# Aligning the entry of three engine programs to an instruction block, in a kernel that streams 268 MB

## The chip, the cores and the metric

One core of a Trainium2 chip. The metric is the device time of one execution in microseconds (us); a kernel is given by the median of its fast executions. The span of a profile runs from the first to the last instruction and is about 1.8 us shorter than the time.

## The reference

```python
B, S, D = 8, 2048, 4096          # x: (8, 2048, 4096) f32, w: (4096, 1) f32

def reference(x, w):
    proj = (x @ w).squeeze(-1)                    # (8, 2048)
    cm = np.maximum.accumulate(proj, axis=1)
    is_record = (proj >= cm).astype(np.float32)
    return np.cumsum(is_record, axis=1).astype(np.float32)
```

So 268 MB of x are read once, each row is reduced to one number, and two short scans follow.

## The kernel before

The first 1920 positions of each batch row are loaded in 32 large pieces (four groups of eight), the last 128 in smaller ones, by SyncE, into a ring of three SBUF buffers of 64 KB per partition. VectorE takes columns 0 to 2815 of each row (multiply and add up in one instruction), Pool multiplies the other 1280 columns and ACT adds them up. TensorE broadcasts w to all partitions at the start and turns the sums into rows; VectorE scans them. VectorE, Pool, ACT and TensorE run the first three groups as a hardware loop of their own (`Fori`).

```python
    with tc.tile_critical(no_gpsimd_drain=True):
        for g in range(NG):
            r = RS[g]
            for t in range(B):
                i = SY.dma_start(out=at(g, t)[:, : r * D], in_=x[...]).then_inc(xs[t], 16)
                u, n = user_before(g, t)
                if n:
                    i._wait_ge(*(free(u, n)))      # the buffer's last user, VectorE and ACT
                if g == t == 0:
                    A.dma_start(                   # w, 16 KB, issued by ACT
                        out=w_row, in_=w.rearrange("(k c) one -> k (c one)", k=NW)
                    ).then_inc(ws, 16)
        # ... cut: stores of the counts, loads of the last 128 positions, constants (Pool), broadcast of w (TensorE, ACT)

        def group_dots(r, g=0):                    # VectorE
            for t in range(B):
                b, xb = B - 1 - t, at(g, t)
                for j in range(r):
                    i = dot(xb[:, j * D : j * D + VC], w_v[:, :VC], sum_v[...])
                    if j == 0:
                        i._wait_ge(xs[t], 16)
                i.then_inc(fr[t], 1)

        with V.Fori(0, NL):
            group_scans()
            V.sem_inc(psr, -3)
            group_dots(R)
        # ... cut: the like loops of Pool, ACT and TensorE, and the tail
```

## Time and profile before

| | before |
|---|---|
| time, three runs | 630.11 us (630.03 to 630.29) |
| span of the profiled run | 629.3 us |
| first x packet starts / last x packet ends | 1.98 / 623.76 us |
| from there to the end | 5.5 us |
| VectorE / Pool / ACT busy | 65% / 59% / 29% |

The profiled run took 631.05 us and so was itself 0.9 us slower than the median; its span should not be compared with others to better than a microsecond.

The page of before: the busy share of the DMA engines in 40 slices of the span (in tenths), and the queues with packets, MB and their share of the time of 16 engines.

```profile
span 629.3 us, 1140 instructions
...
DMA  9999999999999999999999999999999999999996
...
q1 hardware_dynamic: 6544, 268.50, 98.9%
...
q14 instruction: 3, 0.02, 0.0%
```

All 16 DMA engines are busy from the first slice to the last but one: the stream of x is the time. The line q14 counts the instruction blocks that the engines fetched while the kernel ran; three in the whole span.

The waits of before (who waited for whom: us in total, times, longest):

```profile
POOL xall L276 <- DMA xall<-in_x_dram: 243.3, 31, 20.9
DVE xall L124 <- DMA xall<-in_x_dram: 181.8, 30, 7.9
```

The two busiest engines wait for data some thirty times, once per piece.

The timeline of before, first 27 us (start, duration, engine, line, operation, then in brackets the idle time before it and what ended it):

```profile
0.91 0.60 ACTq L178 DMA_DIRECT2D w<-in_w_dram  x1
0.96 0.20 POOL L208 MEMSET identity<- 128x128 f32 x1 [0.51 <-SPq L163]
0.97 1.34 SPq L168 DMA_DIRECT2D xall<-in_x_dram  x3
...
2.62 2.07 PE L224 MATMUL ps<-w,identity 8*128 8x512 f32 x2 [2.62 <-DMA w<-in_w_dram]
...
18.31 0.48 DVE L246 MEMSET ps<- 8x512 f32 x1 [15.71 <-ACT w L235]
...
22.80 3.09 DVE L124 CUSTOM_DVE_ANT_0 xall<-xall,w_v 128x2816 f32<-128x2816 f32 x1 [0.67 <-DMA xall<-in_x_dram]
```

ACT issues w's load just ahead of SyncE's first x load (0.91 against 0.97 us), w's packets are through by 2.10 us, and the first dot is released by the data of x.

The end of the chain of work that ended last (start, duration, what):

```profile
581.81 39.25 DMA xall<-in_x_dram
621.06 0.07 issue
621.13 1.76 POOL xall L336
...
626.10 0.27 DVE cnt L146
```

The last 5 us are the last piece's sums and scans; none of the "issue" steps there is longer than 0.07 us.

### The profile page before, as it was taken

To read this page: it belongs to the slowest core of one execution; us is meant where nothing else is said; L and a number is where in the kernel's file an instruction comes from. 1 tells how busy PE (TensorE), PEld (TensorE's weight loads), DVE (VectorE), ACT (ScalarE), POOL (GpSimd) and SP (SyncE) were. 2 spreads that over 40 slices of the span, in tenths; PEclk is the share of its full clock that TensorE was granted. 3 is DMA by queue.
4 is the path that set the end of the run, shared out by engine and by line. 5 is a ranking of instruction groups with operands and counts; after the bars stand their busy time and mean duration, and the time that the engine had idled before them with its cause. 6 is when DMAs were issued, how large, how long until landed. Compare 5 with 4: busy or idle time off the path is not lost. (4 is left out here: it accounts for less than half of the span.)

```text
span 629.3 us, 1140 instructions
## 1 busy us (share of the span) xinstructions
PE 29.1 (5%) x96; PEld 13.5 (2%) x96; DVE 407.3 (65%) x294; ACT 181.2 (29%) x274; POOL 370.7 (59%) x149
## 2 busy tenths in 40 slices
PE   8000000000020000000001000000002000000100
PEld 3000000000010000000000000000001000000000
DVE  0755775556766567755578655676556976655897
ACT  1222332223322233222233222332223232232254
POOL 0554675456765557745577555676557666555775
PEclk9999999999999999999996555555555555555565
DMA  9999999999999999999999999999999999999996
GB/s 401 400 467 400 446 421 425 442 437 429 442 425 450 417 450 417 459 408 458 408 458 408 458 408 458 408 459 408 462 418 438 416 447 441 413 447 444 404 425 248
DMA packets 6563, 268.54 MB, mean 427 GB/s; under 512 B 760, under 2 KB 1016, under 8 KB 1568
## 3 DMA queue, kind: packets, MB, share of 16 engines
q1 hardware_dynamic: 6544, 268.50, 98.9%
q10 hardware_dynamic: 16, 0.02, 0.0%
q14 instruction: 3, 0.02, 0.0%
HBM read 268.45 MB, written 0.07 MB: 427 GB/s over the span
## 5 line engine op out<-in xcount | busy, mean ns | idle before, releaser
L124 DVE CUSTOM_DVE_ANT_0 xall<-xall,w_v 128x2816 f32<-128x2816 f32 (+1 forms) x129 | 385.5, 3041 | 181.8 <-DMA xall<-in_x_dram 181.8
L276 POOL TENSOR_TENSOR xall<-xall,w_sb 128x1280 f32<-128x1280 f32 x120 | 345.0, 2909 | 246.7 <-DMA xall<-in_x_dram 243.3
L130 ACT ACTIVATE xall<-xall 128x1280 f32<-128x1280 f32 (+2 forms) x130 | 162.9, 1253 | 428.6 <-POOL xall L276 408.3
L312 PE MATMUL ps<-identity,small 128*8 128x128 f32 x60 | 13.0, 406 | 568.6 <-PEq L309 568.6
L130 ACT ACTIVATION_READ_ACCUMULATOR xall<-xall 128x1 f32 x130 | 24.2, 186 | 0.0
L336 POOL TENSOR_TENSOR xall<-xall,w_sb 128x1280 f32<-128x1280 f32 (+2 forms) x8 | 21.1, 2632 | 3.1 <-DMA xall<-in_x_dram 3.0
L312 PEld LDWEIGHTS ps<-identity,small 128*8 128x8 f32 x60 | 7.3, 125 | 575.4 <-issue 571.3
L140 DVE TENSOR_TENSOR_SCAN cm<-ps,cm,small 8x512 f32<-8x512 f32 (+3 forms) x8 | 7.0, 869 | 18.8 <-PE ps L312 18.4
L224 PE MATMUL w_v<-w,identity 8*128 8x512 f32 x14 | 12.1, 1056 | 0.0
L124 DVE DVE_READ_ACCUMULATOR2_ANT small<- 128x1 f32 x133 | 10.8, 81 | 0.0
L246 DVE MEMSET ps<- 8x512 f32 x1 | 0.5, 485 | 15.7 <-ACT w L235 15.7
L146 DVE TENSOR_TENSOR_SCAN cnt<-ps,cnt,small 8x512 f32<-8x512 f32 (+3 forms) x8 | 7.0, 870 | 0.3
L224 PEld LDWEIGHTS w_v<-w,identity 8*128 8x128 f32 x14 | 4.6, 332 | 7.3 <-issue 7.3
L143 DVE TENSOR_TENSOR ps<-ps,cm 8x512 f32<-8x512 f32 (+3 forms) x8 | 3.9, 487 | 0.3
L232 ACT COPY w_sb<-w_v 128x768 f32<-128x768 f32 x1 | 0.8, 799 | 11.4 <-PE w_v L224 11.4
L347 POOL TENSOR_TENSOR masked<-fold,small 128x4 f32<-128x4 f32 x8 | 1.6, 201 | 3.2 <-DVE small L124 3.2
L124 DVE CUSTOM_DVE_ANT_0 xall<-xall,w_v,small 128x480 f32<-128x480 f32 (+2 forms) x4 | 3.1, 810 | 0.2 <-DVE small L124 0.2
L357 PE MATMUL ps<-fold,masked 128*8 128x32 f32 x20 | 2.0, 235 | 25.3 <-ACT masked L352 17.7
L352 ACT ACTIVATE masked<-fold,small 128x4 f32<-128x4 f32 x10 | 3.0, 298 | 0.3
L336 POOL TENSOR_TENSOR xall<-xall,w 128x640 f32<-128x640 f32 (+1 forms) x2 | 2.3, 1137 | 0.1
L224 PE MATMUL ps<-w,identity 8*128 8x512 f32 x2 | 2.1, 1135 | 2.6 <-DMA w<-in_w_dram 2.6
L231 ACT ACT_TABLE_LOAD x1 | 1.3, 1283 | 2.7 <-DVE fold L242 2.7
(18 smaller groups left out, 5.3 us busy)
## 6 DMA issues: line engine op xcount, KB each, us to landing
xall<-in_x_dram SPq DMA_DIRECT2D x8, 6144.0 KB, 33.5
xall<-in_x_dram SPq DMA_DIRECT2D x6, 2048.0 KB, 42.4
xall<-in_x_dram SPq DMA_DIRECT2D x1, 1264.0 KB, 36.6
xall<-in_x_dram SPq DMA_DIRECT2D x1, 816.0 KB, 39.3
xall<-in_x_dram SPq DMA_DIRECT2D x1, 784.0 KB, 37.9
xall<-in_x_dram SPq DMA_DIRECT2D x2, 240.0 KB, 26.6
xall<-in_x_dram SPq DMA_DIRECT2D x1, 416.0 KB, 39.4
xall<-in_x_dram SPq DMA_DIRECT2D x24, 45.0
```

What stands on the lines that cost most here:

```text
L124: return V.tensor_tensor_reduce(out=xsl, in0=xsl, in1=wsl, scale=1.0, scalar=seed, op0=ALU.mult, op1=ALU.add, accum_out=dst,)
L130: return A.activation(out=xsl, in_=xsl, func=ACTF.Copy, accum_out=dst)
L140: V.tensor_tensor_scan(out=cm_, data0=src, data1=low, initial=cm0, op0=ALU.max, op1=ALU.max,)._wait_ge(psr, base).then_inc(psr, 1)
L143: V.tensor_tensor(out=src, in0=src, in1=cm_, op=ALU.is_ge)._wait_ge(psr, base + 1).then_inc(psr, 1)
L146: V.tensor_tensor_scan(out=cnt_, data0=src, data1=low, initial=cnt0, op0=ALU.add, op1=ALU.max,)._wait_ge(psr, base + 2).then_inc(cs, 1)
L224: i = T.matmul(out=dst, lhsT=identity[:NW, k : k + 1].to_broadcast([NW, P]), rhs=w_row, start=True, stop=True,).then_inc(bw, 1)
L276: i = G.tensor_mul(out=xl, in0=xl, in1=w_sb).then_inc(pl, 1)
L312: i = T.matmul(out=ps[:B, j : r * P : r], lhsT=l[:, j * B : (j + 1) * B], rhs=identity, start=k == 0, stop=k == 1,)
L336: G.tensor_mul(out=xl, in0=xl, in1=w_pool(*p))._wait_ge(xq[i], 16).then_inc(pl, 1)
L347: return eng.tensor_tensor(out=e, in0=by_b, in1=acc.to_broadcast([P, H]), op=ALU.mult)
L352: return A.activation(out=e, in_=by_b, func=ACTF.Copy, scale=acc)._wait_ge(pa, na).then_inc(ms, 1)
L357: return T.matmul(out=ps[:B, k * Q : (k + 1) * Q], lhsT=masked[:, n * B : (n + 1) * B], rhs=by_i, start=start, stop=stop,)
```

## The change

The intent: let each engine's loop body lie inside one block of 128 instructions, with a fixed slot for the entry, so that neither back edges nor the tail meet an instruction fetch. `addr_align(128, 2, max_nops=0)` puts the next instruction at slot 2 of a block, by a branch over the gap.

```diff
     def free(u, n):
         return (p7, n) if u == B - 1 else (fr[u], 2 * n)
+
+    for eng in (V, A, G):
+        eng.addr_align(128, 2, max_nops=0)
 
     with tc.tile_critical(no_gpsimd_drain=True):
```

V, A and G are VectorE, ACT and Pool. SyncE and TensorE are left as they were. No other instruction changes; line numbers after it grow by 3.

## The prediction

> **What bounds the kernel now.** The stream of x. The page gives 268.45 MB read in a span of 629.3 us, and every slice but the last has the DMA row at 9. In the trace's packets the first x packet starts 1.98 us after the span's start, the last ends at 623.76 us, and between 2.5 and 622.8 us no 100 ns have fewer than 14 packets in flight on 16 engines. So the time is 2.0 us (entry) + 621.8 us (stream) + 5.5 us (tail: last sums, scans, output, exit). VectorE is busy 65%, Pool 59%, ACT 29%; their waits are for data. The timeline shows slack: the first tile lands at 22.8 us, its buffer is reloaded from 35.8 us, but two more 8.4 MB loads (some 19.5 us each) are then queued, so a buffer may come back over 20 us later before the queue runs dry.
>
> **What the change does.** It moves no arithmetic, load or wait. The VectorE, ACT and Pool programs get one padding instruction ahead of the entry branch, so these three jump to slot 2 of the next block of 128 instructions. The intent: each loop body (about 70, 75 and 36 slots) lies in one block.
>
> *Gain.* No back edge before shows a fetch stall: inside the span the instruction queue carried three 8 KB fetches (at 105.3, 117.4 and 487.6 us, 0.31 us each), none per iteration. There is nothing to save on the path.
>
> *Cost.* One taken branch per engine at about 0.75 us. The Trainium skill, "Runtime: NRT & Kernel Launch", section "Instruction fetch mechanics", says a branch stalls where the target lies outside the current two-page window. The next block should be inside. I read the three fetches as "entering a block fetches the one after", which agrees (the page has 16 KiB blocks, the trace 8 KB packets). So I expect 0.05 to 0.4 us per jump; if the block is missing, 1 to 3 us.
>
> *Critical path.* SyncE does not jump and does not wait for the three: its entry event precedes their branches, and it issues the first x load at 0.97 us. The stream starts at the same time. A late ACT delays the load of w (issued at 0.91 us), w's broadcast, and the first VectorE scans (ending at 22.1 us, 0.7 us ahead of the first tile). Even 3 us there only delays the first dot, and the slack swallows it. In the tail, Pool's program then lies in one block; VectorE and ACT cross once, near the end of the last group, with the block fetched ahead.
>
> **Predicted time:** 630.1 us, 8 in 10 between 629.5 and 630.9. Faster by over 2%: 0.3%; within 2%: 99%; slower by over 2%: 0.7%.
>
> **What would show the steps right.** Span within 0.5 us of 629.3; x stream 1.98 to about 623.8 us; first x load at 0.97 us; w load, copies of w and first dot later by under 0.5 us; three new 8 KB instruction fetches in the first 3 us, none in the loops, then one about 570 to 582 us (ACT) and one about 585 to 598 us (VectorE). Tail chain of the same pieces, 5.5 us. Wrong: the first x load late, a gap in the DMA row, or an "issue" wait of 1 us or more in the last 6 us.
>
> **What would make it wrong.** The jumped-to block is absent and its fetch takes many microseconds behind the x stream; w's load, issued after x has filled the queues, takes over 20 us; the new crossing stalls in the tail; the stream's rate differs on the chip used.

## The result, and the profile after

630.66 us (median of 4 runs, 630.45 to 631.17) against 630.16 us for the kernel before (now 4 runs, 630.03 to 630.29). The ratio is 1.0009, with a 95% interval from 0.9992 to 1.0026: no difference is shown.

The page after:

```profile
span 628.8 us, 1143 instructions
...
DMA  9999999999999999999999999999999999999995
...
q14 instruction: 5, 0.04, 0.0%
```

The three added instructions are the three branches. Five blocks were fetched in the span, where there had been three.

The timeline after, first 32 us:

```profile
0.96 2.12 SPq L171 DMA_DIRECT2D xall<-in_x_dram  x3
1.34 0.20 POOL L211 MEMSET identity<- 128x128 f32 x1 [0.89 <-SPq L166]
1.35 2.38 ACTq L181 DMA_DIRECT2D w<-in_w_dram  x1
...
11.14 2.07 PE L227 MATMUL ps<-w,identity 8*128 8x512 f32 x2 [11.14 <-DMA w<-in_w_dram]
...
26.84 0.48 DVE L249 MEMSET ps<- 8x512 f32 x1 [23.86 <-ACT w L238]
...
30.58 3.05 DVE L124 CUSTOM_DVE_ANT_0 xall<-xall,w_v 128x2816 f32<-128x2816 f32 x1
```

SyncE's first load is issued at the same time as before (0.96 us). ACT now issues w's load 0.4 us later, its issue lasts 2.38 us instead of 0.60, and w arrives 8.5 us later (first broadcast matmul at 11.14 against 2.62 us). The first dot moves from 22.80 to 30.58 us. It is no longer released by x but simply follows the scans.

The waits after, and the end of the chain:

```profile
POOL xall L279 <- DMA xall<-in_x_dram: 218.2, 30, 7.9
DVE xall L124 <- DMA xall<-in_x_dram: 172.9, 28, 7.3
...
DVE ps L249 <- ACT w L238: 23.9, 1, 23.9
```

```profile
581.46 39.13 DMA xall<-in_x_dram
620.60 0.07 issue
620.66 1.75 POOL xall L339
...
625.63 0.27 DVE cnt L146
```

VectorE waits 8.2 us longer for w (23.9 against 15.7 us) and 8.9 us less for data of x (172.9 against 181.8 us): what it lost at the start it took from its own idle time. The x stream ran from 2.00 to 623.29 us, and the end follows 5.5 us later, as before.

The instruction fetches and entry branches, read from the records of the two traces (us from the span's start):

| | before | after |
|---|---|---|
| entry branch: Pool, ACT, VectorE | 0.77, 0.77, 0.79 | 1.15, 1.20, 1.36 |
| added branch: Pool, ACT, VectorE | none | 0.70, 0.74, 0.77 |
| 8 KB fetches | 105.3, 117.4, 487.6 | 1.78, 1.80, 1.95, 559.8, 568.6 |

### The profile page after: what moved, and what is told of

The parts are those of the page before. It is cut to its first block, busy times and chain, and to the rows that moved or that the text cites. A ratio compares the mean times of both kernels' runs of the same rounds, so it can differ in the third digit from the quotient of the medians.

```text
span 628.8 us, 1143 instructions
## 1 busy us (share of the span) xinstructions
PE 29.3 (5%) x96; PEld 13.6 (2%) x96; DVE 407.1 (65%) x294; ACT 181.2 (29%) x274; POOL 370.6 (59%) x149
## 5 line engine op out<-in xcount | busy, mean ns | idle before, releaser
L124 DVE CUSTOM_DVE_ANT_0 xall<-xall,w_v 128x2816 f32<-128x2816 f32 (+1 forms) x129 | 385.4, 3040 | 172.9 <-DMA xall<-in_x_dram 172.9
L249 DVE MEMSET ps<- 8x512 f32 x1 | 0.5, 485 | 23.9 <-ACT w L238 23.9
```

Source lines behind the costliest of these rows:

```text
L124: return V.tensor_tensor_reduce(out=xsl, in0=xsl, in1=wsl, scale=1.0, scalar=seed, op0=ALU.mult, op1=ALU.add, accum_out=dst,)
```

## The experiments

Twelve kernels ran, all of them correct. The 630.66 against 630.16 asked whether half a microsecond had been lost, and the late w asked why.

Theory: the x stream sets the time, the three jumps lie beside it, and whatever they delay is taken from slack. Rivals: the jumps or the late w cost a little that the first runs could not show; the block layout itself matters.

### The changed kernel again

No edit. 

> The changed kernel unaltered, in more rounds, to settle whether its 0.5 us over the kernel before (630.66 against 630.16) is real. Theory (the jumps lie off the path): within 0.05% of before, 630.0 to 630.6 us, x stream from 2.0 us, 621 to 622 us long. Rival (the jumps or the late load of w cost time): 0.08% slower or more, every round the same sign.

Measured: 630.49 us (five runs, 630.40 to 630.92) against 630.31 us (nine runs, 630.11 to 630.89); ratio 1.0002 [0.9988, 1.0016]. The theory's range holds the median, and the runs of the two kernels overlap. No cost of the change is shown; one of 0.1% is not excluded.

### ACT jumps after it has issued w's load

```diff
-    for eng in (V, A, G):
+    for eng in (V, G):
         eng.addr_align(128, 2, max_nops=0)
...
                     A.dma_start(out=w_row, ...).then_inc(ws, 16)
+                    A.addr_align(128, 2, max_nops=0)
```

> VectorE and Pool jump as in the change; ACT jumps only after it has issued the load of w. Theory (w is late because its load was issued at 1.35 us, after the first x load at 0.97 us, and its packets then queue behind x): w issued at 0.9 us, its packets landed by 2.3 us, first broadcast matmul at 2.6 to 3.1 us, as before; time 630.0 to 630.6. Rival (the jump itself delays w): first broadcast matmul near 11 us still. If the 0.5 us of the change came from the late w it is gone here.

Measured: 630.56 us, ratio 1.0003 [0.9989, 1.0017].

```profile
0.92 0.60 ACTq L181 DMA_DIRECT2D w<-in_w_dram  x1
```

w's load was issued at 0.92 us in 0.60 us, the first broadcast matmul came at 3.80 us (0.7 us later than expected; its packets took until 2.84 us in place of 2.10). So w is late because of where its issue stands, not because of VectorE's and Pool's jumps. And an early w does not make the kernel faster: the late w was not the cause of the half microsecond. These runs do not show that it is more than noise.

### w late without any jump

```diff
                 if g == t == 0:
+                    A.wait_ge(con, 7)
                     A.dma_start(out=w_row, ...)
```

> The kernel before without any jump; ACT waits for the constants (about 1.95 us) and only then issues the load of w. Theory (order behind x, not the jump): first broadcast matmul at 9 to 13 us, copies of w at 24 to 27 us, no instruction fetch in the first 20 us, time 630.0 to 630.6. Rival (fetches of instructions hold the load up): first broadcast matmul at 4 us.

Measured: 630.27 us, ratio 0.9997 [0.9983, 1.0011].

```profile
2.03 0.59 ACTq L179 DMA_DIRECT2D w<-in_w_dram  x1
```

ACT issued w at 2.03 us in 0.59 us; the first matmul came at 10.89 us, and there was no fetch in the first 100 us. Being issued behind the first x load is enough to make 16 KB take over 8 us. The trace shows how: w's packets started at 7.57 us, and the short packets that report them done only at 10.06 to 10.28 us, about one x packet (2.42 us) later. The Trainium skill, "DMA: Bandwidth & Descriptors", section "Queues, rings and completion order", says that each DMA engine takes turns between its queues and drains a whole packet before it switches; that agrees with the second step. The first one is 5.5 us from the issue to the packets. In the trace w's packets start when the engines end their second x packet (7.57 to 8.02 us), so two x packets went ahead of w; why two and not one is open.

### Only ACT jumps

```diff
-    for eng in (V, A, G):
+    for eng in (A,):
```

> Only ACT jumps. Theory: one instruction fetch of 8 KB at 1.5 to 2.2 us in place of three, ACT's entry branch at 1.2 us (0.43 us later than before), VectorE's and Pool's at 0.77 to 0.79 us as before; w still late, first broadcast matmul at 9 to 13 us. Of the late fetches one at 555 to 575 us is ACT's; VectorE and Pool keep two of the three of before. Span 628.3 to 629.5.

Measured (one run, state unknown): 630.24 us, span 628.4 us. One fetch near the start (1.80 us), ACT's entry branch at 1.20 us, VectorE's and Pool's at 0.79 and 0.77; first matmul at 10.85 us. The late fetches came at 104.5, 486.9 and 568.5 us: the last is ACT's, and so the one that is gone (117.4 us) was ACT's before. All as expected, but for one thing. ACT's issue of w took 2.28 us here, with no other engine jumping:

```profile
1.35 2.28 ACTq L181 DMA_DIRECT2D w<-in_w_dram  x1
```

That suggested that an engine's first load after it enters a block is held up by that engine's own fetch. It is not simply a wait for the fetch: its packet was done at 2.47 us, and the issue ended at 3.63 us. It matters for the engine that starts the stream.

### SyncE jumps as well

```diff
-    for eng in (V, A, G):
+    for eng in (SY, V, A, G):
```

> SyncE jumps as well. Theory (a jump costs 0.4 to 0.6 us and matters only on the engine that starts the stream of x): first x load issued at 1.35 to 1.5 us instead of 0.97, first x packet at 2.35 to 2.55 us, stream 621 to 622 us, tail 5.5 us, so the span 0.4 to 0.6 us above the changed kernel's, 630.7 to 631.1 us. ACT now issues w about as early as SyncE issues x, so the first broadcast matmul comes at 3 to 5 us again. Rival (jumps cost nothing, the delays of the other engines had other causes): x issued at 0.97 us.

Measured: 633.37 us, ratio 1.0045 [1.0031, 1.0059]: 3.1 us slower, not 0.5. SyncE issued its first x load at 1.46 us, as expected, but the issue took 2.51 us instead of 0.40, and the first x packet started at 4.58 us. The stream (621.6 us) and the tail (5.5 us) kept their lengths. The direction was right: on this engine a jump costs the whole kernel. The size was not: I had counted the jump and left out the fetch.

### SyncE alone jumps, to a new block and inside its block

```diff
-    for eng in (V, A, G):
-        eng.addr_align(128, 2, max_nops=0)
+    SY.addr_align(128, 2, max_nops=0)        # the first of the two kernels
+    SY.addr_align(128, 100, max_nops=0)      # the second, in its place
```

> Only SyncE jumps to the next block. Theory (the first load that an engine issues right after entering a block waits for that engine's own 8 KB fetch): SyncE's first x load is issued near 1.46 us and its issue takes 2.2 to 2.7 us instead of 0.40, first x packet at 4.3 to 4.8 us, time 632.6 to 633.5 us. ACT's issue of w takes 0.6 us. Rival (the four fetches of four engines and ACT's stretched issue crowd it): issue 0.4 to 0.8 us, first x packet at 2.4 to 2.9 us, time 630.7 to 631.3.

> Only SyncE jumps, but to slot 100 of the block that it is in, so no new block is entered. Theory (the fetch costs, not the branch): no fetch by it in the first 3 us, first x load issued at 1.05 to 1.25 us, issue 0.40 us, first x packet 2.05 to 2.25 us, time 630.3 to 630.8. Rival (any jump ahead of the first load costs 2 to 3 us): 632.5 us or more.

Measured: into a new block 632.32 us, ratio 1.0029 [1.0015, 1.0043]; inside the block 630.43 us, ratio 0.9999 [0.9985, 1.0012]. With the new block the first load was issued at 1.46 us, its issue took 1.85 us, and the first x packet started at 3.93 us. The start of the issue is as expected; the other two are a little under it (and the time too), but nearer to the theory than to the rival. ACT, which did not jump, issued w in 0.60 us, as expected. The fetch's packet was done at 2.12 us and SyncE's issue ended at 3.31 us, so what fills the time between is not shown. Inside the block there was no fetch at the start, the issue took 0.40 us, and x started at 2.20 us. So the branch costs 0.2 us and entering the new block the rest. The difference to the kernel where four engines jump (1.85 against 2.51 us) says that the fetches also crowd one another, or ACT's load crowds SyncE's; which, is open.

The stretch from 2 to 4 us, first of the kernel where SyncE alone enters a new block, then of before (window, length, busy us of PE, PEld, DVE, ACT, POOL, granted clock, DMA share, GB/s):

```profile
2.00:4.00 2.00, 0.97 (x1) 0.49 (x2) 0.57 (x2) 0.81 (x1) 0.42 (x6) 1.00 0.63 205
```

```profile
2.00:4.00 2.00, 1.38 (x2) 0.82 (x3) 0.57 (x2) 1.28 (x1) 0.00 (x0) 1.00 1.44 492
```

205 GB/s against 492: the first packets of x are missing. (A share over 1 comes from packets that overlap on an engine.)

### Two blocks ahead

```diff
     for eng in (V, A, G):
         eng.addr_align(128, 2, max_nops=0)
+        eng.addr_align(128, 1, max_nops=0)
```

> Each of the three jumps twice, to slot 2 of the next block and from there to slot 1 of the block after. Theory (the next block is there at entry, the one after is fetched only when the next is entered): the second jump waits for the 8 KB fetch of 1.8 to 2.4 us, entry branches at 2.3 to 3.5 us; w's load lands at 9 to 12 us; the x stream still starts at 2.0 us and the time is 630.0 to 630.7. Rival 1 (a jump costs its branch alone, wherever it goes): entry branches at 1.6 to 1.9 us. Rival 2 (the missing block is fetched behind x): 5 to 10 us.

Measured: the second jumps ended at 3.45 (ACT), 3.52 (Pool) and 3.80 us (VectorE), 2.3 to 2.5 us after the first ones. So the next block was there at entry, and the one after had to be fetched (at 1.8 us). ACT's issue of w then took 6.0 us, w landed at 17.2 us (9 to 12 had been expected), and the first dot came at 37.06 us. But the time was 631.26 us, ratio 1.0015 [1.0002, 1.0029]: 0.97 us slower, where I had expected nothing. The x stream started on time (1.98 us) and lasted 621.89 us, with the tail at 5.5 us. (The profile of before has 621.8 us, but that run was 0.9 us slow; the other kernels that kept their time have 620.9 to 621.3 us.) The late w is not it: an experiment below has a later first dot (39.8 us) at no cost. Near the end of the stream:

```profile
622.50:623.70 1.20, 0.00 (x0) 0.00 (x0) 1.20 (x3) 0.66 (x1) 1.11 (x2) 0.50 0.14 52
```

A DMA share of 0.14 is about two engines of 16 still moving x; the others are done. In the trace, three more fetches lie inside the stream (at 7.7 us), and beside each of them one x packet is 0.52 to 0.62 us longer than its neighbours. The same is seen in before: at the fetch of 105.3 us one packet of x took 2.96 us where its neighbours took 2.42. This is the theory that the last experiment tests.

### Loops over a block edge, and an edge in the tail

```diff
-    for eng in (V, A, G):
-        eng.addr_align(128, 2, max_nops=0)
+    for eng, slot_ in ((V, 91), (A, 92), (G, 40)):
+        eng.addr_align(128, slot_, max_nops=0)
```

> Entry slots 91 (VectorE), 92 (ACT), 40 (Pool) in place of 2: the loops of VectorE and ACT straddle a block edge, and all three engines cross an edge within the last 10 us, on the chain that ends the kernel. Theory (the block ahead is fetched one block early, and a body over an edge stays resident): three fetches near 1.8 us, two at 50 to 110 us, two or three at 610 to 628 us, none per iteration; from the end of the last x packet to the end 5.4 to 5.7 us as before and after; time 630.0 to 630.7. Rival (layout matters): a fetch per iteration, or a tail of 6.5 to 10 us, and 631.5 us or more.

Measured: 630.42 us, ratio 1.0002 [0.9989, 1.0016]; fetches at 2.04, 46.4, 77.6, 587.8, 606.3 and 624.2 us, none per iteration; tail 5.57 us. VectorE and ACT turned out to jump inside the block that they were in (entry 0.2 us after the added branch, one fetch at the start instead of three). The late fetches came somewhat earlier than I had said, the last within the last 5 us. Here ACT issued w at 1.05 us, only 0.08 us behind the first x load, and the first matmul still came at 8.44 us. The layout that the change was to avoid costs nothing measurable.

### w later still

```diff
+                    A.wait_ge(con, 2)
+                    for q in range(3):            # 8 in the second kernel
+                        d = A.copy(out=w_v, in_=identity[:, :1].to_broadcast([P, CV]))
+                        if q:
+                            d._wait_ge(dl, q)
+                        d.then_inc(dl, 1)
+                    A.wait_ge(dl, 3)              # 8
                     A.dma_start(out=w_row, ...)
```

Both are the kernel before, without a jump; the idle copies only pass time.

> The kernel before, no jump; ACT makes three idle copies into the buffer of w ahead of w's load. Theory (slack of the three-buffer ring): w issued at 13 to 16 us, first dot at 40 to 47 us, over 9 us later than in the changed kernel, the first buffer's reload issued 13 us after the first dot, still before the queue is empty at 61.5 us; time unchanged, 630.0 to 630.7. Rival (lateness of w is passed on): the time grows by a microsecond or more.

> The same with eight idle copies. Theory: first dot at 60 to 67 us; the queue of x runs dry once the third tile has landed at 61.5 us and starts again about 14 us after the first dot, so one gap in the DMA row of (first dot - 47.5) us, give or take 1.5, 13 to 19 us, and the time is 630.3 us plus that gap, 643 to 650 us; nothing is lost later. Rival (no such edge, the ring never runs dry): 630.0 to 631 us.

Measured, three copies: w issued at 11.7 us, first dot at 39.83 us (both a little under what I had expected), 630.26 us, ratio 1.0001 [0.9986, 1.0016]. The first dot is 17 us later than before and the time is the same.

Measured, eight copies: first dot at 54.49 us, earlier than expected (a copy took 3.18 us), so the times expected in numbers, 643 to 650 us, were missed. The rule that was written beside them gives 54.5 - 47.5 = 7.0 us of gap. The gap was 6.9 us (60.8 to 67.7 us with fewer than 14 packets in flight), and the time 638.32 us against 630.32 us, ratio 1.0123 [1.0107, 1.0140]: 8.0 us more. The gap, in the eight-copy kernel and in the same stretch of before:

```profile
60.80:67.80 7.00, 0.00 (x0) 0.00 (x0) 7.00 (x5) 2.75 (x5) 7.00 (x3) 1.00 0.40 131
```

```profile
60.80:67.80 7.00, 0.00 (x0) 0.00 (x0) 5.79 (x3) 1.36 (x2) 5.74 (x3) 1.00 1.04 449
```

So the slack has an edge. A first dot up to about 47 us is free (an estimate: 54.5 less the 7 us of gap); past it, in the one kernel that went there, 7.0 us of lateness cost 8.0 us. The changed kernel, at 30.6 us, stands 17 us ahead of it.

### Many blocks in the loop

```diff
             for t in range(B):
                 b, xb = B - 1 - t, at(g, t)
+                V.addr_align(128, 2, max_nops=0)
                 for j in range(r):
```

> The kernel before; VectorE jumps to the next block ahead of every tile, 8 times a loop iteration, so its loop runs over 8 blocks and fetches through the whole stream. Theory (a fetch inside the stream makes one x packet 0.53 us longer and that DMA engine stays behind, VectorE's fetches all go to one DMA engine): 24 to 36 fetches, x stream longer by 0.53 us each, 12 to 19 us, time 642 to 650 us, VectorE itself still waiting for data at every tile. Theory b (the fetches are spread over the engines): 0.8 to 2 us longer, 631 to 632.5. Rival (fetches cost the stream nothing; the 0.97 us of the kernel with two jumps came from elsewhere): 630.0 to 630.8.

Measured: 664.23 us, ratio 1.0533 [1.0519, 1.0548], 33.7 us slower. VectorE still waited for data in total longer than before (214.6 against 181.8 us), so it was not the one that was slow. Its wait, two page lines, and a stretch near the end:

```profile
DVE xall L124 <- DMA xall<-in_x_dram: 214.6, 30, 9.0
...
DMA  9999999999999999999599999999999899999960
...
q14 instruction: 38, 0.31, 0.1%
```

```profile
645.00:655.00 10.00, 0.38 (x4) 0.20 (x4) 8.85 (x15) 5.36 (x11) 8.04 (x8) 0.50 0.06 26
```

38 blocks (24 to 36 had been expected), 0.31 MB, cost 33.7 us. In the last stretch the share is 0.06, one engine of 16, at 26 GB/s: one DMA engine finishes the stream alone. Its last x packet ends at 656.94 us. That is theory a, one DMA engine that falls behind with each fetch, and not the spreading of theory b. The size was taken too small: beside most fetches the x packet was 0.65 us longer, and the fetch itself took 0.31 us; I had counted only the first kind, at 0.53. The pieces of x then came every 20.3 us where they had come every 19.4 us.

The kept traces do not name the DMA engine of a packet. But in a full stream the next packet of an engine starts within some 12 ns of the end of its last one, so the packets can be followed from end to start, and a fetch is seen between two x packets of one engine. Followed so, 34 of the 38 fetches lie on one engine, the one that ends at 656.94 us; the others are done by 641 us. That is 33.7 us for 34 fetches, 0.99 us each, close to the 0.96 us of the two parts.

The same reading explains the 0.97 us of the kernel that went two blocks ahead. Its three fetches at 7.7 us lie on three different engines, which end at 622.91, 623.48 and 623.88 us; the other thirteen end between 621.7 and 622.2 us. The two that end last are the ones that also carry the late fetches (560.4 and 567.5 us). So two fetches add up on one engine, where the changed kernel has one.

It also shows something that the first profiles hid. In before, the engines that carried the fetches of 117.4, 487.6 and 105.3 us end at 623.43, 623.44 and 623.76 us, the other thirteen at 622.6 to 623.0 us. In after, the two with the late fetches end at 622.76 and 623.29 us, the others at 621.9 to 622.4 us. In 13 of the 14 traces the engine that ends the stream had carried a fetch (in that of the jump inside SyncE's block two engines cannot be told apart). So even one fetch sets the end of the stream back, by some 0.9 us in before.

## Why the prediction was right

- **The stream sets the time: shown.** In all 14 traces the tail after the last x packet is 5.5 to 5.6 us. The changed kernel is 2.0 + 621.3 + 5.5 us. Every kernel that was slower had a later start of the stream (3.93 and 4.58 us) or a longer stream (621.9, 629.0 and 654.9 us). The others have 620.9 to 621.3 us, except the profile of before with its 621.8 us, taken in a run that was 0.9 us slow.
- **SyncE does not jump, so the stream starts as before: shown.** The first x packet started at 1.98 before and 2.00 us after. Where SyncE jumps into a new block, it starts at 3.93 or 4.58 us and the kernel loses 1.8 or 3.1 us.
- **The slack swallows a late start of VectorE, ACT and Pool: shown**, up to a first dot at 39.8 us; and the edge is shown too, at about 47 us.
- **No back edge paid a fetch before, so back edges had nothing to give: shown.** A kernel whose loops were laid to cross an edge has no fetch per iteration and the same time.
- **Overlooked: the few late fetches are on the path.** The prediction listed them and gave them no cost. Each sets one DMA engine back, and the stream ends with such an engine, before and after. In both kernels that engine carries one fetch inside the stream, so the cost stayed about the same; this was not foreseen, and to that extent the close hit is luck. By the same account a kernel with no fetch inside the stream would end some 0.9 us earlier (an estimate from the ends of the engines in before; not tried).
- **The next block is there at entry: shown.** The first jumps took 0.44 to 0.59 us (added branch to entry branch; I had said 0.05 to 0.4), while a second jump took 2.3 to 2.5 us. The Trainium skill, "Runtime: NRT & Kernel Launch", section "Instruction fetch mechanics", says that a branch stalls where its target is outside the current two-page window. These numbers agree.
- **Wrong: "w load, copies of w and first dot later by under 0.5 us".** They came 7.8 to 8.5 us later. I had costed the branch alone. In the trace the order of two issues turned around: w's load had been 0.05 us ahead of the first x load and then came 0.4 us behind it, and behind x it took 8 us more. It was named among the things that could go wrong, and it could not cost time below some 17 us more.
- **Wrong in part: the late fetches.** One was expected at 570 to 582 us (ACT) and one at 585 to 598 us (VectorE). They came at 568.6 and 559.8 us. ACT's is told apart by the kernel where ACT alone jumps; the other is VectorE's by exclusion, as Pool's section was counted to fit one block. I took an engine's place in its program from the instruction that it executes; VectorE's loop branch is recorded at 467.8 us, with eight instructions of the loop still to finish, so the program runs ahead. That explains a part of the 25 us; the rest is open.
- **Not settled: whether the change costs 0.1%.** The two sets of runs give 1.0009 and 1.0002, and both intervals hold 1. A few tenths of a microsecond remain possible: in the three profiles where VectorE and Pool jump to a new block and the time is the same (after, its repeat, and the one with w ahead of ACT's jump) the stream lasted 621.25 to 621.34 us, in five others of the same time 620.9 to 621.1 us.

## What to carry to other kernels

Ask first which engine starts the work that bounds the kernel: three engines could be moved by half a microsecond, and w by 8.5, at no cost that was measured, while the same branch on the queue that starts the stream cost 1.8 to 3.1 us. When a change delays an issue by even 0.4 us, check what it now stands behind; a small load that loses its place to a big one can pay far more than the delay (here 8.5 us for 0.4). In a kernel whose DMA engines are always full, code that is fetched during the stream is not free: each 8 KB block set one DMA engine back by some 0.6 to 1.2 us (the ends of the engines above), blocks of one engine's program added up on one DMA engine, and the stream ends with its slowest engine.

## What the Trainium skill lacked or had wrong

- "Runtime: NRT & Kernel Launch", section "Instruction fetch mechanics", gives refills in blocks of 16 KiB (256 instructions). Here each jump into a new block brought one fetch of 8 KB (128 instructions of the 64 bytes that "Perfetto Trace Analysis", section "The 4-stage abstract model", gives): three jumping engines three packets, one engine one.
- The same section calls the cost of crossing a block "mostly hidden". For the engine that crosses, these runs agree (tail 5.57 us with a fetch in its last 5 us, against 5.50 us). But it has nothing on the cost to a full DMA stream: 34 fetches on one DMA engine made the kernel 33.7 us slower, 0.99 us each.
- No page that I read says that an engine's first DMA issue after entering a new block is stretched: 2.28 to 2.63 us on ACT where it had been 0.60, and 1.85 us on SyncE where it had been 0.40 (2.51 us with the other engines jumping too); 6.0 us on ACT after two blocks.
- "DMA: Bandwidth & Descriptors", section "Queues, rings and completion order", has the turns between queues, but not what they add up to for a small load: 16 KB of w were used at 2.62 us when issued 0.05 us ahead of x, at 8.44 us when issued 0.08 us behind it, and at 10.89 us when issued at 2.03 us, with x packets of 2.42 us.
- The same page, section "Specifications", gives some 358 GB/s as the HBM limit of a core. This core read at 427 GB/s over the whole span. Further down the page measures 425 GB/s for a core whose neighbour is idle, which fits; so the row is not wrong, but it lacks that condition.
